# Strassen's seven products summed in three PSUM banks, with ScalarE copies in place of VectorE additions

## The chip, the core and the metric

The kernel runs on one core of a Trainium2 chip. The metric is the device time of one execution in microseconds (us). Engines are named as the profile names them: PE is TensorE (matmul), PEld its weight load, DVE VectorE, ACT ScalarE, POOL GpSimd, SP SyncE (which only issues DMAs here).

## What is computed

A transformer block in float32: T = 2048 tokens, width D = 1024, D_FF = 2816. The first two thirds (input projection, attention, pooling mixer, output projection) are not touched. The change lies in the gated MLP at the end, on the normalised tokens h:

```
u = h @ w_up                                   # (2048, 1024) @ (1024, 5632)
u = up[:-2]*conv_w[0] + up[1:-1]*conv_w[1] + up[2:]*conv_w[2] + conv_b   # along the tokens
gate, val = u[..., :D_FF], u[..., D_FF:]
return (silu(gate) * val) @ w_down             # (2048, 2816) @ (2816, 1024)
```

## The kernel before

Each float32 operand of a matmul is split into a high and a low part, and a product is the sum of three matmuls: high x high, high x low, low x high. The splits are a cast on ScalarE (`wh_*`, `gh`, `wdh`) and a subtraction on GpSimd or VectorE (`wl_*`, `gl`, `wdl`).

**Parts and units.** The MLP works through the tokens in three parts (`PARTS`): 640, 768 and 640 tokens. For each part it goes through 22 units j; a unit computes 128 columns of the gate half and 128 of the value half of `u`, as a 2x2 block product: two halves of the contraction, the gate and the value block of w_up on the stationary side, two halves of the tokens (N = 322, 386, 322 columns) on the moving side. Winograd's form of Strassen's product needs seven products, named 1 to 7, of 12 matmuls each (four blocks k of 128 rows by three splits; L1156), on sums of blocks: s1 to s4 of the weights, t1 to t4 of the tokens.

**The seven products before.** Each has a bank of its own out of five `pp` banks in turn, in the order 1, 6, 2, 7, 5, 4, 3. ScalarE copies product 1 to `p1s` (L1163). VectorE adds the rest: w1 = 6 + p1s (L1165), c11 = 2 + p1s (L1167), w7 = 7 + w1 (L1169), c22 = 5 + w7 (L1171), w1 = 5 + w1 (L1172), c21 = w7 - 4 (L1174), c12 = 3 + w1 (L1176). c11 and c12 are the two token halves of the gate block `ug`, c21 and c22 those of the value block `uv`.

**What runs beside a unit.** The loop in which a unit's matmuls are written steps other generators, so that their instructions stand between: `gen_w` prepares the weights of the next unit (casts on ScalarE L1033, sums and subtractions on GpSimd L1035 to L1055; seven buffers for the seven operands); `gen_gate` does the convolution and gate of the unit before (ScalarE L1199, VectorE L1202 and L1205 for each half, silu L1208, the product of the halves on VectorE L1212, its split `gh` on ScalarE L1219 and `gl` on VectorE L1221); `gen_down` multiplies the gate of unit j-2 with w_down, five or six token tiles by two column halves, each a group of three matmuls into one of three `py` banks (L1233), emptied by a VectorE addition to `y` (L1238; the first group of a part by a copy on ScalarE, L1236). Only in part 1, VectorE also multiplies w_down by the gate vector (`wds`, L56) and splits it (L1123, with ScalarE L1122). In units 2 to 6 of part 1 one VectorE addition of 128x1024 brings in the residual (L1312); in parts 2 and 3 halves of it (L1257). The first unit of parts 2 and 3 (`kmajor`) runs its seven products side by side over k; the second unit has no down-projection between its products, which begins with the third.

Each engine carries out its instructions in the order in which they were put on it; a scheduler sets that order by the program's dependences, so that an edit in `gen_up` also moves what stands beside it. A bank or buffer is written again when its last reader is done.

Of the kernel before, what the change touches and what calls it, by code (L numbers as in the profile page):

```python
# [14 lines left out]
ALU = mybir.AluOpType  # L15
# [32 lines left out]
class InOrder:  # L48
    """An engine whose instructions stay in the order in which they are written."""
# [15 lines left out]
def hybrid_block(ctx: ExitStack, tc: tile.TileContext, x, c, w_ada, b_ada, norm1_g, w_in,  # L65
# [58 lines left out]
    # =============== mixer input projection ===============  # L124
    with tc.tile_pool(name="p1", bufs=1) as p1, \
            tc.tile_pool(name="ps1", bufs=1, space=PSUM) as ps1:
        # columns of w_in: q, k, v first (their space is free first), then u
# [173 lines left out]
        # scale and shift of the first norm; the first tokens' norm beside them  # L301
# [18 lines left out]
        # weights, split, in the order of use  # L320
# [19 lines left out]
        # 1/count at the clipped edges  # L340
# [108 lines left out]
        def gen_tr(tok, qhl, khl):  # L449
            """q as (hi, lo), k as (hi, hi) and (lo, one), transposed"""  # L450
# [25 lines left out]
        def windows(b, us, res):  # L476
            """column i is token t0 - 8 + i, at column 8 + i of u; the last block has 8 more"""
# [74 lines left out]
        def gen_early_max():  # L552
            """the row maxima of the first unit over the keys of the blocks that are done"""
# [75 lines left out]
    # =============== attention and output projection ===============  # L629
    ctx3 = ctx.enter_context(ExitStack())  # L630
    with tc.tile_pool(name="po", bufs=1, side="right", reuse_waits="tile") as po, \
# [8 lines left out]
        # per key tile: [v_lo 0 | v_hi 0 | ones | v_hi 1 | v_lo 1]  # L640
# [185 lines left out]
        def gen_out(c_, half, wait=0):  # L826
            """x1 = x + pool half, then x1 += attention half."""
# [17 lines left out]
        def gen_ln2(t, x1, junk, hts, bank, stat, wait):  # L845
            """normalised x1, transposed"""
# [31 lines left out]
        # the last chunk's output projection: the pool half first, in banks that the attention leaves  # L878
# [67 lines left out]
        # =============== gated conv MLP: Winograd's form of Strassen's product ===============  # L946
# [12 lines left out]
        def gen_ops(p, res):  # L959
            """the moving operands of part p, split"""  # L960
# [10 lines left out]
            for k in range(4):  # L971
# [35 lines left out]
                G.tensor_tensor(out=t2, in0=t2, in1=b21, op=ALU.subtract)  # L1007
# [7 lines left out]
        def gen_w(p, j, res):  # L1015
            """the stationary operands of one pair of column tiles, split, in the order of use"""
# [22 lines left out]
            yield  # L1039
            s1, s2 = raw2(f"s1_{p}_{j}"), raw2(f"s2_{p}_{j}")  # L1040
# [3 lines left out]
            yield  # L1044
            split("a12", a12)
# [54 lines left out]
    with tc.tile_pool(name="p3", bufs=1, reuse_waits="tile") as p3, \  # L1100
# [5 lines left out]
        def gen_wd(p, j, n, tag=""):  # L1106
            """w_down times the gate, split: worked out with the first part, kept in DRAM for the others"""
# [18 lines left out]
            else:  # L1126
# [7 lines left out]
        PROD = (("1", "a11", "b11"), ("6", "s2", "t2"), ("2", "a12", "b21"), ("7", "s3", "t3"),  # L1134
                ("5", "s1", "t1"), ("4", "a22", "t4"), ("3", "s4", "b22"))

        def gen_up(p, j, kmajor, res):
            o0, no, N = PARTS[p]
# [5 lines left out]
            w1 = p3.tile([P, 386], F32, tag="w1", name=f"w1{p}_{j}", bufs=1)[:, 0:N]  # L1144
            w7 = p3.tile([P, 386], F32, tag="w7", name=f"w7{p}_{j}", bufs=1)[:, 0:N]
            res.append((p, j, ug, uv))

            def bank(i):
                py = kmajor and i < 2
                return ps3_.tile([P, 512], F32, tag="py" if py else "pp", name=f"pp{PROD[i][0]}{p}_{j}",  # L1150
                                bufs=3 if py else 5)[:, 0:N]

            def prod(ps, i, k):
                (ah, al), (bh, bl) = w[PROD[i][1]], o[PROD[i][2]]
                for m, (l_, r_) in enumerate(((ah, bh), (ah, bl), (al, bh))):
                    mm = PE.matmul(ps, l_[:, k], r_[:, k, 0:N], start=k == 0 and m == 0, stop=k == 3 and m == 2)  # L1156
                    if kmajor:
                        tc.keep_in_program_order(mm)
                    yield

            def add(i, ps):
                if i == 0:
                    S.copy(out=p1s, in_=ps)  # L1163
# [14 lines left out]
            if kmajor:  # L1178
# [4 lines left out]
                for i in range(7):  # L1183
                    add(i, banks[i])
# [226 lines left out]
```

## Time and profile before

| | |
|---|---|
| median of 3 runs | 2740.19 us (2736.31 to 2745.56) |
| span of the profiled execution | 2741.8 us |
| TensorE busy | 2594.1 us (95%) |
| VectorE busy | 2370.5 us (86%) |
| ScalarE busy | 1475.5 us (54%) |
| GpSimd busy | 1767.0 us (64%) |
| MLP, part 1 from its first unit | from 1283 us |
| 12 steady units of part 1 | 1478.41 to 1731.10 us |
| 17 steady units of part 2 | 1842.02 to 2235.18 us |
| 17 steady units of part 3 | 2378.57 to 2706.33 us |

No separate device time of the profiled execution is recorded; its span stands for it. A start is in us from the beginning of the span. Instructions of one engine overlap at their ends, so the distance from one start to the next can be shorter than an instruction.

### The profile page before, as it was taken

How to read it: one execution, taken by the hardware profiler on the slowest of the kernel's cores; microseconds unless marked ns; L12 is line 12 of the kernel's file. 1: busy time of each engine (PE TensorE's matmuls, PEld its weight loads, DVE VectorE, ACT ScalarE, POOL GpSimd, SP SyncE). 2: the span in 40 equal slices, each digit the busy share in tenths (PEclk: the TensorE clock that was granted, in tenths of full speed). 3: DMA queues.
4: the chain of work that ended last, by engine and by line, in shares of the span. 5: the costliest groups of instructions: out<-in, count | busy, mean ns of one | idle time of the engine just before them, and what ended most of it. 6: DMA issues, size and time to landing. Idle time of an engine off the chain costs nothing.

```text
span 2741.8 us, 39488 instructions
## 1 busy us (share of the span) xinstructions
PE 2594.1 (95%) x13439; PEld 2242.1 (82%) x13439; DVE 2370.5 (86%) x3526; ACT 1475.5 (54%) x2656; POOL 1767.0 (64%) x1397
## 2 busy tenths in 40 slices
PE   5899989999999999999899999899999998999999
PEld 5788867777776767767888888789999997999998
DVE  7778688989999998887999999978888888898886
ACT  5566457777778777775533443543333334533342
POOL 1222146556657666565888888697777776988883
PEclk9899989999999999999999999999999999999999
DMA  9685374331221222225444444443333224433332
GB/s 291 232 258 179 99 239 149 106 95 60 64 80 55 71 72 76 80 64 179 151 130 133 128 130 123 145 132 105 100 104 100 93 87 132 147 123 120 106 110 93
DMA packets 318164, 338.65 MB, mean 124 GB/s; under 512 B 24655, under 2 KB 226329, under 8 KB 317961
## 3 DMA queue, kind: packets, MB, share of 16 engines
q1 hardware_dynamic: 316953, 332.31, 38.4%
q0 software_dynamic: 1008, 3.81, 0.5%
q8 instruction: 106, 1.74, 0.3%
q14 instruction: 97, 0.79, 0.1%
HBM read 249.42 MB, written 86.63 MB: 123 GB/s over the span
## 4 chain that ended last, share of the span: by engine, by line
PE 36%; DVE 13%; issue 3%; ACT 1%; POOL 1%; POOLq 0%; DVEq 0%; ACTq 0%
PE pp L1156 23%; PE py L1233 13%; DVE y L1238 3%; DVE ac L1202 2%; DVE ac L1205 2%; DVE b L993 1%; DVE t L993 1%; ACT ac L1199 1%; PE pl L1354 1%; DVE wds L56 0%; DVE wdl L1123 0%; DVE ac L1212 0%; DVE ug L1176 0%; DVE uv L1171 0%; DVE uv L1174 0%
## 5 line engine op out<-in xcount | busy, mean ns | idle before, releaser
L1035 POOL TENSOR_TENSOR wl_s<-s,wh_s 128x512 fp32r<-128x512 f32 x260 | 390.3, 1502 | 187.8 <-ACT wh_s L1033 186.6
L1238 DVE TENSOR_TENSOR y<-py,y 128x512 f32<-128x512 f32 x620 | 418.5, 682 | 95.5 <-PE py L1233 94.8
L741 POOL TENSOR_TENSOR acc<-acc,ph 128x512 f32<-128x512 f32 x352 | 463.4, 1316 | 41.0 <-ACT ph L735 15.7
L1156 PE MATMUL pp<-t,wh_s 128*128 128x322 f32 (+1 forms) x1584 | 390.2, 322 | 7.0 <-DVE x L1072 3.2
L737 DVE TENSOR_TENSOR pl<-S,ph 128x512 fp32r<-128x512 f32 x512 | 348.7, 684 | 38.5 <-ACT S L736 31.5
L735 ACT ACTIVATE ph<-S 128x512 fp32r<-128x512 f32 x512 | 307.3, 600 | 131.9 <-PE S L732 116.2
L694 DVE TENSOR_REDUCE mx<-pmx 128x1 f32<-128x512 f32 x500 | 338.1, 681 | 27.0 <-PE pmx L692 25.2
L1035 POOL TENSOR_TENSOR wl_a<-wr,wh_a 128x512 fp32r<-128x512 f32 x195 | 312.9, 1605 | 22.7 <-ACT wh_a L1033 22.6
L1233 PE MATMUL py<-wdh,gh 128*128 128x512 f32 x674 | 275.7, 409 | 47.1 <-DVE y L1238 40.6
L736 ACT ACTIVATE S<-S 128x512 f32<-128x512 f32 x512 | 306.4, 598 | 0.0
L1156 PEld LDWEIGHTS pp<-t,wh_s 128*128 128x128 f32 x1584 | 282.2, 190 | 27.8 <-DVE t L993 4.1
L1033 ACT CAST wh_s<-s 128x512 fp32r<-128x512 f32 x264 | 161.9, 617 | 226.8 <-PE pp L1156 197.0
L1156 PE MATMUL pp<-b,wh_a 128*128 128x322 f32 (+1 forms) x1056 | 267.9, 323 | 1.3 <-DVE b L993 0.8
L1233 PE MATMUL py<-wdh,gl 128*128 128x512 f32 x674 | 268.8, 399 | 0.0
L1233 PE MATMUL py<-wdl,gh 128*128 128x512 f32 x674 | 268.8, 399 | 0.0
L1156 PE MATMUL pp<-t,wl_s 128*128 128x322 f32 (+1 forms) x792 | 254.3, 321 | 0.0
L724 PE MATMUL B<-pl,vt 128*128 128x512 f32 x512 | 210.5, 411 | 6.2 <-DVE pl L737 6.0
L1033 ACT CAST wh_a<-wr 128x512 fp32r<-128x512 f32 x198 | 122.3, 618 | 165.6 <-PE pp L1156 158.4
L723 PE MATMUL A<-ph,vt 128*128 128x512 f32 x512 | 204.7, 408 | 5.2 <-ACT ph L735 5.2
L692 PE MATMUL pmx<-kA,qa 128*128 128x512 f32 x500 | 203.3, 408 | 3.9 <-DMA kA<-k_scr 3.0
L739 POOL TENSOR_TENSOR acc<-ph,ph 128x512 f32<-128x512 f32 x32 | 41.3, 1290 | 256.8 <-ACT ph L735 226.9
L732 PE MATMUL S<-qb,kB 65*128 65x512 f32 x512 | 202.8, 402 | 1.1 <-ACT qb L702 0.8
(273 smaller groups left out, 6784.4 us busy)
## 6 DMA issues: line engine op xcount, KB each, us to landing
wr<-in_w_up_dram SPq DMA_DIRECT2D x132, 512.0 KB
wdh<-wd_scr SPq DMA_DIRECT2D x88, 256.0 KB
wdl<-wd_scr SPq DMA_DIRECT2D x88, 256.0 KB
stage<-in_w_ada_dram SPq DMA_DIRECT2D x36, 512.0 KB
x_scr<-x SPq DMA_DIRECT2D x48, 256.0 KB
wds<-in_w_down_dram SPq DMA_DIRECT2D x44, 256.0 KB
wd_scr<-wdh SPq DMA_DIRECT2D x44, 256.0 KB
wd_scr<-wdl SPq DMA_DIRECT2D x44, 256.0 KB
```

The costliest lines, as they stand in the source:

```text
L694: V.tensor_reduce(out=mx[:, qt, j:j + 1], in_=ps, axis=AX.X, op=ALU.max)
L723: PE.matmul(A, vt[:, kt, 192 * a:192 * a + P], ph, start=kt == 0, stop=kt == NKT - 1)
L724: PE.matmul(B, vt[:, kt, 64 + 64 * a:192 + 64 * a], pl, start=kt == 0, stop=False)
L735: S.activation(out=ph, in_=s, func=AF.Exp, scale=0.125)
L736: S.activation(out=s, in_=s, func=AF.Exp, scale=0.125)
L737: V.tensor_tensor(out=pl, in0=s, in1=ph.bitcast(F32), op=ALU.subtract)
L741: G.tensor_tensor(out=acc, in0=acc, in1=ph.bitcast(F32), op=ALU.add)
L1033: S.copy(out=hf, in_=src)
L1035: eng.tensor_tensor(out=lf, in0=src, in1=hf.bitcast(F32), op=ALU.subtract)
L1156: mm = PE.matmul(ps, l_[:, k], r_[:, k, 0:N], start=k == 0 and m == 0, stop=k == 3 and m == 2)
L1233: PE.matmul(ps, l_[:, ts_], r_, start=i == 0, stop=i == 3 * len(js) - 1)
L1238: V.tensor_tensor(out=ys[t][:, ns], in0=ps, in1=ys[t][:, ns], op=ALU.add)
```

## The change

A unit uses three banks, X, Y and W, and lets TensorE do four of the sums by accumulating on what a bank already holds: X takes product 1, then 6, then 5, then 3; W takes 7, then 4; Y takes 2. The values are read out between: X after 1 is `p1s`; X after 6 is 1 + 6, copied to `u2s`; W after 7 is copied to `w7`; X after 5 is 1 + 6 + 5, to which VectorE adds w7 for c22; W after 4 is added to u2s for c21; X after 3 is c12, copied straight to `ug`. The operand t4 changes its sign, so that product 4 is added. The order of products becomes 1, 2, 6, 7, 5, 4, 3, and `gen_w` prepares a12 ahead of s2. Units with `kmajor` keep seven banks and the old sums.

```
# gen_ops
-                G.tensor_tensor(out=t2, in0=t2, in1=b21, op=ALU.subtract)
+                G.tensor_tensor(out=t2, in0=b21, in1=t2, op=ALU.subtract)
# gen_w
+            split("a12", a12)
+            yield
             s1, s2 = raw2(f"s1_{p}_{j}"), raw2(f"s2_{p}_{j}")
             E.tensor_tensor(out=s1, in0=a21, in1=a22, op=ALU.add)
             E.tensor_tensor(out=s2, in0=s1, in1=a11, op=ALU.subtract)
             split("s2", s2)
-            yield
-            split("a12", a12)
             yield
# gen_up
+            def prod(ps, nm, k, first=True):
+                (ah, al), (bh, bl) = w[PROD[nm][0]], o[PROD[nm][1]]
                 for m, (l_, r_) in enumerate(((ah, bh), (ah, bl), (al, bh))):
+                    mm = PE.matmul(ps, l_[:, k], r_[:, k, 0:N], start=first and k == 0 and m == 0,
+                                   stop=k == 3 and m == 2, skip_group_check=not first)
...
-            else:
-                for i in range(7):
-                    ps = bank(i)
-                    for k in range(4):
-                        yield from prod(ps, i, k)
-                    add(i, ps)
+            X, Y, W = bank("x"), bank("y"), bank("w")
+
+            def run(ps, nm, first):
+                for k in range(4):
+                    yield from prod(ps, nm, k, first)
+
+            yield from run(X, "1", True)
+            S.copy(out=p1s, in_=X)
+            yield from run(Y, "2", True)
+            add(c11, Y, p1s)
+            yield from run(X, "6", False)
+            S.copy(out=u2s, in_=X)
+            yield from run(W, "7", True)
+            S.copy(out=w7, in_=W)
+            yield from run(X, "5", False)
+            add(c22, X, w7)
+            yield from run(W, "4", False)
+            add(c21, W, u2s)
+            yield from run(X, "3", False)
+            S.copy(out=c12, in_=X)
```

How this moves instructions is seen on two engines. First ScalarE in a steady unit of part 1 (j = 4), from the copy of product 1 to the last weight cast; in a name the number behind the tile's name is the part, then the unit. Before:

```order
L1163 COPY p1s0_4_14927<-pp10_4_14930 128x322
L1208 ACTIVATE ac00_3_14939<-ac00_3_14939 128x640
L1033 CAST wh_s20_5_14993<-s2_0_5_14990 128x512
L1122 CAST wdh0_3_0_15013<-wds0_3_0_14921 128x512
L1219 CAST gh0_3_15072<-ac00_3_14939 128x640
L1033 CAST wh_a120_5_15021<-wr0_5_0_14934 128x512
L1122 CAST wdh0_3_1_15085<-wds0_3_1_14923 128x512
L1033 CAST wh_s30_5_15055<-s3_0_5_15053 128x512
```

And with the change (the line numbers are those of the changed kernel: L1187, L1191 and L1193 are the three copies, L1217 silu, L1228 the gate's high part `gh`):

```order
L1187 COPY p1s0_4_14907<-ppx0_4_14910 128x322
L1217 ACTIVATE ac00_3_14921<-ac00_3_14921 128x640
L1033 CAST wh_a120_5_14969<-wr0_5_0_14916 128x512
L1122 CAST wdh0_3_0_14989<-wds0_3_0_14901 128x512
L1228 CAST gh0_3_15050<-ac00_3_14921 128x640
L1033 CAST wh_s20_5_15001<-s2_0_5_14998 128x512
L1191 COPY u2s0_4_14908<-ppx0_4_14910 128x322
L1122 CAST wdh0_3_1_15063<-wds0_3_1_14903 128x512
L1033 CAST wh_s30_5_15034<-s3_0_5_15032 128x512
L1193 COPY w70_4_14909<-ppw0_4_14912 128x322
```

The cast of a12 now stands ahead of `gh` and that of s2 behind it; behind that comes the copy of X to `u2s`, and two casts later that of W to `w7`.

Second, VectorE in the same unit, from the sum with product 7 to that with product 4. Before (L1312 is the residual, L1238 a sum of the down-projection):

```order
L1169 TENSOR_TENSOR w70_4_14929<-pp70_4_15032,w10_4_14928 128x322
L1238 TENSOR_TENSOR y0_1_14465<-py0_2_1_1_15065,y0_1_14465 128x512
L1238 TENSOR_TENSOR y0_2_14466<-py0_2_2_1_15092,y0_2_14466 128x512
L1171 TENSOR_TENSOR uv0_4_14926<-pp50_4_15061,w70_4_14929 128x322
L1172 TENSOR_TENSOR w10_4_14928<-pp50_4_15061,w10_4_14928 128x322
L1312 TENSOR_TENSOR y0_2_14466<-y0_2_14466,xr0_4_15037 128x1024
L1238 TENSOR_TENSOR y0_3_14467<-py0_2_3_1_15109,y0_3_14467 128x512
L1174 TENSOR_TENSOR uv0_4_14926<-w70_4_14929,pp40_4_15101 128x322
```

And the same stretch with the change (L1164 is the addition of `gen_up`, L1247 a sum of the down-projection, L1321 the residual):

```order
L1247 TENSOR_TENSOR y0_1_14455<-py0_2_1_1_15043,y0_1_14455 128x512
L1247 TENSOR_TENSOR y0_2_14456<-py0_2_2_1_15070,y0_2_14456 128x512
L1164 TENSOR_TENSOR uv0_4_14906<-ppx0_4_14910,w70_4_14909 128x322
L1321 TENSOR_TENSOR y0_2_14456<-y0_2_14456,xr0_4_15016 128x1024
L1247 TENSOR_TENSOR y0_3_14457<-py0_2_3_1_15085,y0_3_14457 128x512
L1164 TENSOR_TENSOR uv0_4_14906<-ppw0_4_14912,u2s0_4_14908 128x322
```

The sums w7 and w1 are gone; c22 is added from bank X, with the residual behind it, and c21 from bank W.

## Rows read from the trace of the kernel before

**Rows 1.** The head of the page: span, then busy time, share, instructions

```profile
span 2741.8 us, 39488 instructions
...
PE 2594.1 (95%) x13439; PEld 2242.1 (82%) x13439; DVE 2370.5 (86%) x3526; ACT 1475.5 (54%) x2656; POOL 1767.0 (64%) x1397
```

**Rows 2.** Stage windows: us, busy of PE, PEld, DVE, ACT, POOL, PEclk

```profile
1347.08:1478.41 131.33, 118.40 (x674) 106.94 (x675) 129.34 (x166) 51.32 (x86) 112.65 (x68) 1.00 0.45 139
1478.41:1731.10 252.69, 238.92 (x1373) 217.30 (x1373) 247.98 (x325) 102.53 (x170) 206.63 (x133) 1.00 0.41 125
...
2378.57:2706.33 327.76, 327.76 (x1934) 306.07 (x1934) 291.76 (x400) 131.35 (x205) 279.99 (x188) 1.00 0.35 110
```

**Rows 3.** TensorE's waits in part 1 (total, times, longest)

```profile
PE py L1233 <- DVE y L1238: 26.7, 36, 1.5
```

**Rows 4.** VectorE's waits in twelve steady units of part 1

```profile
DVE ac L1202 <- ACT ac L1199: 4.7, 12, 0.4
```

**Rows 5.** VectorE's groups in the same units: times, busy, mean ns

```profile
L1212 DVE TENSOR_TENSOR ac<-ac,ac 128x640 f32<-128x640 f32 x12 | 21.8, 1815 | 0.0
...
L1165 DVE TENSOR_TENSOR w<-pp,p1s 128x322 f32<-128x322 f32 x12 | 5.8, 482 | 0.0
```

**Rows 6.** VectorE's timeline, one unit of part 1: start, length, instruction

```profile
1600.12 0.48 DVE L1174 TENSOR_TENSOR uv<-w,pp 128x322 f32<-128x322 f32 x1
...
1603.24 1.51 DVE L1205 SCALAR_TENSOR_TENSOR ac<-uv,cols,ac 128x640 f32<-128x640 f32 x1
...
1606.51 1.77 DVE L56 TENSOR_TENSOR wds<-wds,gate 128x512 f32<-128x512 f32 x1
...
1608.81 0.87 DVE L1205 SCALAR_TENSOR_TENSOR ac<-ug,cols,ac 128x640 f32<-128x640 f32 x1
...
1610.20 0.68 DVE L56 TENSOR_TENSOR wds<-wds,gate 128x512 f32<-128x512 f32 x1
1610.80 0.48 DVE L1165 TENSOR_TENSOR w<-pp,p1s 128x322 f32<-128x322 f32 x1
1611.20 1.82 DVE L1212 TENSOR_TENSOR ac<-ac,ac 128x640 f32<-128x640 f32 x1
```

**Rows 7.** ScalarE's timeline in the same unit

```profile
1604.75 0.42 ACT L1163 COPY p1s<-pp 128x322 f32<-128x322 f32 x1
...
1613.05 0.73 ACT L1219 CAST gh<-ac 128x640 fp32r<-128x640 f32 x1 [1.52 <-DVE ac L1212]
1613.68 0.62 ACT L1033 CAST wh_a<-wr 128x512 fp32r<-128x512 f32 x1
```

**Rows 8.** TensorE's timeline: first matmuls of products, one down

```profile
1802.77 0.52 PE L1156 MATMUL pp<-t,wh_s 128*128 128x386 f32 x2
...
1823.22 0.80 PE L1233 MATMUL py<-wdh,gh 128*128 128x512 f32 x1 [2.90 <-ACT y L1236]
...
2330.93 0.45 PE L1156 MATMUL pp<-t,wh_s 128*128 128x322 f32 x2
...
2580.11 0.46 PE L1156 MATMUL pp<-t,wh_s 128*128 128x322 f32 x2
...
2585.71 0.47 PE L1156 MATMUL pp<-b,wh_s 128*128 128x322 f32 x2
```

**Rows 9.** VectorE's timeline, a unit of part 3: c21

```profile
2585.91 0.49 DVE L1174 TENSOR_TENSOR uv<-w,pp 128x322 f32<-128x322 f32 x1
```

**Rows 10.** GpSimd: one group in part 1's steady units, then a timeline row

```profile
L1035 POOL TENSOR_TENSOR wl_s<-s,wh_s 128x512 fp32r<-128x512 f32 x48 | 74.6, 1553 | 39.7 <-ACT wh_s L1033 39.7
...
1611.04 1.30 POOL L1035 TENSOR_TENSOR wl_s<-s,wh_s 128x512 fp32r<-128x512 f32 x1 [3.31 <-ACT wh_s L1033]
```

**Rows 11.** ScalarE's timeline: gh in units of parts 2 and 3

```profile
1807.69 0.84 ACT L1219 CAST gh<-ac 128x768 fp32r<-128x768 f32 x1 [0.62 <-DVE ac L1212]
...
2330.85 0.73 ACT L1219 CAST gh<-ac 128x640 fp32r<-128x640 f32 x1
...
2576.60 0.73 ACT L1219 CAST gh<-ac 128x640 fp32r<-128x640 f32 x1 [1.11 <-DVE ac L1212]
```

More of the change, by code (lines that the diff above doesn't have):

```diff
@@ L1133, in hybrid_block @@
         G1, O0, O1, O2 = 2, 0, 1, 3
-        PROD = (("1", "a11", "b11"), ("6", "s2", "t2"), ("2", "a12", "b21"), ("7", "s3", "t3"),
-                ("5", "s1", "t1"), ("4", "a22", "t4"), ("3", "s4", "b22"))
+        PROD = {"1": ("a11", "b11"), "6": ("s2", "t2"), "2": ("a12", "b21"), "7": ("s3", "t3"),
+                "5": ("s1", "t1"), "4": ("a22", "t4"), "3": ("s4", "b22")}
         def gen_up(p, j, kmajor, res):
@@ L1143, in gen_up, with bank @@
             p1s = p3.tile([P, 386], F32, tag="p1s", name=f"p1s{p}_{j}", bufs=1)[:, 0:N]
-            w1 = p3.tile([P, 386], F32, tag="w1", name=f"w1{p}_{j}", bufs=1)[:, 0:N]
+            u2s = p3.tile([P, 386], F32, tag="w1", name=f"u2s{p}_{j}", bufs=1)[:, 0:N]
             w7 = p3.tile([P, 386], F32, tag="w7", name=f"w7{p}_{j}", bufs=1)[:, 0:N]
             res.append((p, j, ug, uv))
[L1148 to L1154, printed above, removed]
+            c11, c12, c21, c22 = ug[:, 0:N], ug[:, N:2 * N], uv[:, 0:N], uv[:, N:2 * N]
+            def bank(nm, tag="pp"):
+                return ps3_.tile([P, 512], F32, tag=tag, name=f"pp{nm}{p}_{j}",
+                                 bufs=3 if tag == "py" else 5)[:, 0:N]
+            def prod(ps, nm, k, first=True):
+                (ah, al), (bh, bl) = w[PROD[nm][0]], o[PROD[nm][1]]
                 for m, (l_, r_) in enumerate(((ah, bh), (ah, bl), (al, bh))):
-                    mm = PE.matmul(ps, l_[:, k], r_[:, k, 0:N], start=k == 0 and m == 0, stop=k == 3 and m == 2)
+                    mm = PE.matmul(ps, l_[:, k], r_[:, k, 0:N], start=first and k == 0 and m == 0,
+                                   stop=k == 3 and m == 2, skip_group_check=not first)
                     if kmajor:
@@ L1159, in prod, with add @@
                     yield
[L1161 to L1176 removed]
+            def add(out, ps, b):
+                V.tensor_tensor(out=out, in0=ps, in1=b, op=ALU.add)
@@ L1178, in gen_up @@
             if kmajor:
-                banks = [bank(i) for i in range(7)]
+                banks = {nm: bank(nm, "py" if i < 2 else "pp") for i, nm in enumerate("1627543")}
                 for k in range(4):
-                    for i in range(7):
-                        yield from prod(banks[i], i, k)
-                for i in range(7):
-                    add(i, banks[i])
-            else:
-                for i in range(7):
-                    ps = bank(i)
-                    for k in range(4):
-                        yield from prod(ps, i, k)
-                    add(i, ps)
+                    for nm, ps in banks.items():
+                        yield from prod(ps, nm, k)
@@ new lines, in gen_up @@
+                S.copy(out=p1s, in_=banks["1"])
+                add(u2s, banks["6"], p1s)
+                add(c11, banks["2"], p1s)
+                add(w7, banks["7"], u2s)
+                add(c22, banks["5"], w7)
+                add(u2s, banks["5"], u2s)
+                add(c21, banks["4"], w7)
+                add(c12, banks["3"], u2s)
+                return
+            X, Y, W = bank("x"), bank("y"), bank("w")
+            def run(ps, nm, first):
+                for k in range(4):
+                    yield from prod(ps, nm, k, first)
```

12 lines of the change are left out of this document (removed).

## The prediction

> **What bounds the kernel now.** The page's head first [rows 1]: TensorE is busy for 95% of the span, VectorE for 86%. That is an average over stages, so next come the stage windows [rows 2]. In the steady stretch of part 3 TensorE is busy without a gap (327.76 of 327.76 us) and VectorE is not (291.76); part 2, with its wider products, is of the same kind. Nothing that only unloads VectorE can gain there. Seventeen units of part 3 take 327.76 us, 19.28 each, and this is the matmul time of a unit of 322 columns. Part 1 has the same matmuls and is another case. Its twelve steady units take 252.69 us, 21.06 each, with VectorE busy for 247.98 of them and TensorE for 238.92. Its six units ahead of these take 131.33, 21.89 each, with VectorE busy for 129.34. The waits agree: in part 1 TensorE stands 26.7 us in 36 waits, all for the y additions that empty the py banks [rows 3], and VectorE idles 4.7 us in twelve units, all for ScalarE [rows 4]. So VectorE sets the pace of 18 units, TensorE that of the rest, and the change can earn only in part 1: 12 x (21.06 - 19.28) + 6 x (21.89 - 19.28) = 37 us at the very most.
>
> **What it takes from VectorE.** Four additions a unit leave it (L1165, L1169, L1172, L1176), busy for 0.48 us each by L1165's mean [rows 5], but overlapped with the next: from the start of L1165 to that of L1212 it is 1611.20 - 1610.80 = 0.40 [rows 6]. All four have the same 322 columns, so 1.6 us together. VectorE's own sum falls to 21.06 - 1.6 = 19.46 us, still a hair above TensorE's 19.28.
>
> **What it gives ScalarE.** Three copies more a unit, at the 0.42 us of the p1s copy [rows 7]: 1.3 us on an engine that is busy 102.53 us in twelve units (8.5 of 21 us each) [rows 2]. The load is nothing. TensorE's own instructions are the same in number and length.
>
> **What it adds: four waits on TensorE.** Each bank is written again one product after it was read. X+=6 waits for the p1s copy, W+=4 for the w7 copy, X+=3 for the VectorE addition c22, and in each case the reader has a product's time, with the downs between, to be done. The one that matters is X+=5, behind u2s, because of what stands ahead of u2s on ScalarE: gh and wh_s2 (the ScalarE order above). gh waits for the product of the two gate halves on VectorE (L1212 before), which ends the convolution of the unit before, which begins with that unit's c21. So a ring closes: c21, convolution, gh, u2s, products 5 and 4, c21 again. I work out its length in part 1. From the start of c21 (1600.12) to gh (1613.05) it is 12.93 us [rows 6, 7]; the c12 addition that VectorE has in between (0.40) goes, so 12.53. gh to the next start is 0.63, the cast behind it 0.62, the copy 0.42 [rows 7]: 1.67, in whose full lengths the signals are contained. From the start of product 5 to that of product 3 TensorE needs 2585.71 - 2580.11 = 5.60 us where it does not wait [rows 8], and c21 starts 0.20 us after that [rows 9]. Sum: 12.53 + 1.67 + 5.60 + 0.20 = 20.0 us. This is above 19.46, so the ring and not VectorE's sum sets the new pace. It contains two-input VectorE work that stretches when GpSimd works beside it: L1212 takes 1815 ns on average in part 1, while L1205, as large, takes 0.87 us at 1608.81, where GpSimd is idle: its instruction at 1611.04 starts after 3.31 us of waiting [rows 5, 6, 10]. I add 0.3 us for such shifts: **20.3 us**. The bounds of the unit are 19.46 (no ring) and 21.8 (rival D).
>
> The gain of part 1: 12 x (21.06 - 20.3) = 9.1 us. The six units ahead carry the addition of the residual too, between c22 and c21, inside the ring's TensorE leg; by 0.3 us more than the plain ones, 20.6: 6 x (21.89 - 20.6) = 7.7. Together 16.8 us.
>
> **The same wait in parts 2 and 3.** In a steady unit of part 3 gh starts at 2576.60 and product 5 at 2580.11 [rows 8, 11]: u2s would be done 1.7 us after gh, 1.8 us early; here a second cast of 0.62 us comes ahead of it, so 1.2. No wait. In part 2, with 386 columns in place of 322, product 5 comes later still. The second unit of each part is different: it has no down-projection between its products, so product 5 comes early, while gh hangs on a first unit whose sums all come late. In part 2 product 5 starts at 1802.77 and gh at 1807.69 [rows 8, 11]; u2s would end at 1809.4, and TensorE stand 6.6 us. Much is given back, since today it stands 2.90 us a little later for the first y copies [rows 8], and catches up against work that is there anyway: I take 2 us (bounds 0 and 6.6). In part 3 it is 2330.93 against 2330.85 + 1.7 [rows 8, 11]: 1.6 us. The start of part 1 gets 0.5, and the three ends of parts, whose gate chain loses the 0.40 us of c12 each, give 1.2 back. Net cost: 2 + 1.6 + 0.5 - 1.2 = 2.9 us.
>
> **Sum.** The profiled execution's span is 2741.8 us [rows 1], 1.6 above the median of the three runs, 2740.19. 2741.8 - 16.8 + 2.9 = 2727.9 on the profile's basis; less part of the 1.6 that the profile lies high, **2727 us**.
>
> **The Trainium skill against the trace.** What the trace shows: the 1.82 us of L1212 begin 0.16 us into a GpSimd subtraction of 1.30 us [rows 6, 10], whose mean in twelve units is 1.55 us [rows 10]; VectorE and GpSimd together are busy for 247.98 + 206.63 us in 252.69 [rows 2], far more than the stretch: the two do run at once, slowed, and not only by turns. The Trainium skill's page "SBUF — State Buffer" (section "Who interferes with whom") states that a VectorE instruction with two SBUF inputs and a GpSimd instruction that reads SBUF hold a shared port by turns, and that the loser blocks for the whole instruction. By that rule time that VectorE gets free goes to waiting for GpSimd, and part 1 hardly shortens; the trace agrees in that L1205 is short where GpSimd is idle, and not in the full exclusion. It makes rival C.
>
> **The rivals.**
> B, the ring does not bind: u2s comes in time, since the shorter unit leaves the convolution less to share with GpSimd. For it: half a us of the ring is all that decides. Units take 19.46, and 20.29 with a residual: 18 x 1.6 = 28.8 saved, 2.9 lost, about 2715 us.
> C, nothing comes of it: the additions that leave read one of their inputs from PSUM, keep their 0.48 us on average [rows 5] and are not the work that stretches; all of that is left. GpSimd's 17.2 us a unit is then packed against less VectorE time, and a unit stays at 20.9 to 21. By the formula below that gains 4 to 6 us, against a cost of 2.9: 2738 us.
> D, the other side: the ring is longer than I have it. Its convolution contains an L1205 of 0.87 us and a wds of 0.68 that were short since GpSimd idled there; their fellows beside GpSimd take 1.51 and 1.77 [rows 6]. If GpSimd, whose work for the next unit now comes in another order (a12 ahead of gh on ScalarE, s2 behind it), fills that hole and idles elsewhere, the two stretch by 0.64 and 1.09 us, and the ring is 21.8 us. With 0.3 more for the six units ahead, as above, part 1 gains 12 x (21.06 - T) + 6 x (21.59 - T) at a unit of T; from T = 21.1 on that no longer pays the 2.9 us, and the change costs time. At 21.8 it loses 10.1, with the 2.9 13 us: 2754; at 21.5, 7.6: 2748. I put D at 2750.
>
> **How the numbers follow.** Chances: forecast (2722 to 2734) 0.45, B 0.20, C 0.19, D 0.16. What a measurement of this kernel can tell from no change is about 0.3%, 8.2 us: faster is below 2732, slower above 2748. Of the forecast 0.4 of 0.45 is faster, and with B's 0.2, less a little for its tail, 0.57; slower is D, less its lower end, and the tail of C where the second unit of part 2 pays its full wait, 0.14; the rest 0.29. The range for 8 in 10 goes from a little under B, 2712, to where C ends and D begins, 2745.
>
> **What would show it.** In the trace of the changed kernel: TensorE waits in part 1 put down to ScalarE's u2s (or to the pp bank behind it), about 0.9 us a unit, with the y waits of [rows 3] mostly gone; VectorE idle, about 0.8 us a unit; units of about 20.3 us, and unchanged 19.3 us in part 3; one wait of several us in the second unit of part 2. If units of part 1 are at 19.5, B is right; if VectorE is as busy as before with longer convolution instructions, C; if the u2s waits are over 1.5 us a unit, D. The forecast is wrong altogether if the banks' other three waits show up in every unit of parts 2 and 3, which have no room for any.

## The result, and the profile after

The changed kernel takes 2761.93 us (median of 4 runs, 2761.34 to 2775.07), the kernel before 2739.31 beside it: a ratio of 1.0089, 95% interval 1.0064 to 1.0113. It is slower by 23 us, where 2727 was forecast.

The head of the changed kernel's page, as in [rows 1] (the span, then busy time, share and instructions):

```profile
span 2759.4 us, 39247 instructions
...
PE 2593.6 (94%) x13439; PEld 2246.9 (81%) x13439; DVE 2310.2 (84%) x3270; ACT 1548.8 (56%) x2848; POOL 1749.2 (63%) x1397
```

VectorE lost 256 instructions and 60 us of busy time, and the span grew by 17.6 us. The changed kernel's first unit began 4.5 us earlier than before's, which the edit does not touch, so from there on it lost 22.1. The copy of product 1 to p1s comes once a unit, so its starts can serve as marks. Between marks at units where they stand alike in both programs, part 1 loses 6.1 us, and the two changes from part to part lose 7.3 and 7.1:

```
                                               before    changed
first copy to unit 9 of part 1                 193.29     196.17   +2.9
nine steady units of part 1                    189.50     192.71   +3.2
unit 18 of part 1 to unit 4 of part 2          196.92     204.25   +7.3
sixteen steady units of part 2                 370.35     370.98   +0.6
unit 20 of part 2 to unit 5 of part 3          162.65     169.77   +7.1
sixteen units of part 3                        308.50     309.47   +1.0
```

Stage windows of the changed kernel (columns as in [rows 2]): nine steady units of part 1, and the second unit of part 3:

```profile
1476.79:1669.50 192.71, 177.03 (x1028) 162.99 (x1027) 187.91 (x208) 87.79 (x155) 153.18 (x100) 1.00 0.40 123
2339.49:2354.73 15.24, 14.77 (x78) 14.54 (x79) 9.16 (x9) 8.50 (x17) 12.80 (x10) 0.79 0.34 115
```

A steady unit is 192.71 / 9 = 21.41 us, against 21.06 before. VectorE is recorded as busy for 187.91 of the 192.71 us, with 1.6 us of additions less in each unit. TensorE's waits from the MLP's first unit to the end (answer to [rows 3], which covers part 1):

```profile
PE ppx L1157 <- ACT u2s L1191: 44.5, 24, 6.2
PE py L1242 <- DVE y L1247: 10.8, 13, 2.2
PE ppx L1157 <- ACT p1s L1187: 8.7, 3, 5.2
```

The y waits of part 1 are gone, and 53 us of waits for the copies u2s and p1s have come, the u2s waits of the nine steady units being 15.7 of them. Three of them on TensorE's timeline: one of a steady unit of part 1, and those of the second units of parts 2 and 3:

```profile
1615.41 0.57 PE L1157 MATMUL ppx<-t,wh_s 128*128 128x322 f32 x2 [1.73 <-ACT u2s L1191]
...
1814.65 1.01 PE L1157 MATMUL ppx<-t,wh_s 128*128 128x386 f32 x2 [6.23 <-ACT u2s L1191]
...
2339.96 0.91 PE L1157 MATMUL ppx<-t,wh_s 128*128 128x322 f32 x2 [5.24 <-ACT p1s L1187]
```

And what ScalarE did in the first and the last of these places (answer to [rows 7]):

```profile
1610.46 0.74 ACT L1217 ACTIVATE ac<-ac 128x640 f32<-128x640 f32 x1 [4.77 <-DVE ac L1214]
1611.10 0.60 ACT L1033 CAST wh_a<-wr 128x512 fp32r<-128x512 f32 x1
...
1613.79 0.73 ACT L1228 CAST gh<-ac 128x640 fp32r<-128x640 f32 x1 [1.51 <-DVE ac L1221]
1614.42 0.61 ACT L1033 CAST wh_s<-s 128x512 fp32r<-128x512 f32 x1
1614.94 0.42 ACT L1191 COPY u2s<-ppx 128x322 f32<-128x322 f32 x1
...
2338.34 0.74 ACT L1217 ACTIVATE ac<-ac 128x640 f32<-128x640 f32 x1 [7.28 <-DVE ac L1214]
2338.98 0.60 ACT L1033 CAST wh_a<-wr 128x512 fp32r<-128x512 f32 x1
2339.49 0.42 ACT L1187 COPY p1s<-ppx 128x322 f32<-128x322 f32 x1
```

In part 1 u2s (1614.94) stands behind gh and wh_s2, as the prediction said. In part 3 p1s (2339.49) stands behind silu, which waits 7.28 us for the convolution; the prediction saw this only for u2s.

Next, VectorE's and GpSimd's timelines in the same unit of part 1, as [rows 6, 10]:

```profile
1607.28 1.31 DVE L1211 SCALAR_TENSOR_TENSOR ac<-ug,cols,ac 128x640 f32<-128x640 f32 x1
...
1609.11 1.31 DVE L1214 SCALAR_TENSOR_TENSOR ac<-ug,cols,ac 128x640 f32<-128x640 f32 x1
...
1611.55 0.48 DVE L1164 TENSOR_TENSOR ug<-ppy,p1s 128x322 f32<-128x322 f32 x1
1611.95 1.80 DVE L1221 TENSOR_TENSOR ac<-ac,ac 128x640 f32<-128x640 f32 x1
```

```profile
1607.87 1.88 POOL L1035 TENSOR_TENSOR wl_a<-wr,wh_a 128x512 fp32r<-128x512 f32 x1
1611.78 1.29 POOL L1035 TENSOR_TENSOR wl_a<-wr,wh_a 128x512 fp32r<-128x512 f32 x1 [2.04 <-ACT wh_a L1033]
1615.11 1.30 POOL L1035 TENSOR_TENSOR wl_s<-s,wh_s 128x512 fp32r<-128x512 f32 x1 [2.04 <-ACT wh_s L1033]
```

Read the two together. GpSimd's operation of 1611.78 ends at 1613.07. VectorE's product of the halves (L1221) starts at 1611.95 and ends at 1613.75: 0.68 us after that. It was on the engine for 1.80 us, and as a run below shows it needs 0.81 alone. The same at 1609.11: GpSimd ends at 1607.87 + 1.88 = 1609.75, VectorE at 1610.42, 0.67 later. And the other way round: GpSimd's operation of 1607.87 starts while VectorE's L1211 runs, which ends at 1608.59; it takes 1.88 us where the next takes 1.29, and ends 1.16 after L1211. Whoever comes second waits, and the wait is recorded as busy.

All of the nine units' trace is like this. 72 VectorE instructions with both operands in SBUF start while a GpSimd operation runs, with 0.62 to 1.24 us of it left, and end 0.68 us (54 of 128x640: 0.677 to 0.685) or 0.55 us (18 of 128x512: 0.546 to 0.552) after it, however much was left. The 18 others start while GpSimd stands and take 0.67 to 0.68 us. 54 GpSimd operations start while such an instruction runs and end 1.15 to 1.17 us after it; the 45 others take 1.29 to 1.30. So the two take turns, and in what follows a turn is such an instruction of either engine.

GpSimd itself stands twice a unit, for casts that ScalarE has behind silu and behind gh (waits of the nine units):

```profile
POOL wl_a L1035 <- ACT wh_a L1033: 18.4, 9, 2.0
POOL wl_s L1035 <- ACT wh_s L1033: 18.3, 9, 2.0
```

And VectorE's groups, first in the twelve steady units of before (more of the view of [rows 5]), then in these nine:

```profile
L1123 DVE TENSOR_TENSOR wdl<-wds,wdh 128x512 fp32r<-128x512 f32 x24 | 23.4, 976 | 0.0
...
L1205 DVE SCALAR_TENSOR_TENSOR ac<-uv,cols,ac 128x640 f32<-128x640 f32 x12 | 18.1, 1510 | 0.0
...
L1221 DVE TENSOR_TENSOR gl<-ac,gh 128x640 fp32r<-128x640 f32 x12 | 15.8, 1313 | 0.0
L1205 DVE SCALAR_TENSOR_TENSOR ac<-ug,cols,ac 128x640 f32<-128x640 f32 x12 | 10.4, 870 | 0.0
```

```profile
L1123 DVE TENSOR_TENSOR wdl<-wds,wdh 128x512 fp32r<-128x512 f32 x18 | 22.1, 1228 | 0.0
L1221 DVE TENSOR_TENSOR ac<-ac,ac 128x640 f32<-128x640 f32 x9 | 16.3, 1808 | 0.0
L1214 DVE SCALAR_TENSOR_TENSOR ac<-uv,cols,ac 128x640 f32<-128x640 f32 x9 | 16.2, 1805 | 0.3
L1230 DVE TENSOR_TENSOR gl<-ac,gh 128x640 fp32r<-128x640 f32 x9 | 14.5, 1608 | 0.0
...
L1214 DVE SCALAR_TENSOR_TENSOR ac<-ug,cols,ac 128x640 f32<-128x640 f32 x9 | 11.8, 1312 | 0.0
```

The second step of the convolution is L1205 before and L1214 now: 1510 and 1805 ns for the value half, 870 and 1312 for the gate half. The product of the halves (L1212 before, L1221 now) keeps its 1.81 us; wdl and gl are longer as well.

### The profile page after: what moved, and what is told of

Same layout as the page of the kernel before. It is cut to its first block, busy times and chain, and to the rows that moved or that the text cites. A ratio compares the mean times of both kernels' runs of the same rounds, so it can differ in the third digit from the quotient of the medians.

```text
span 2759.4 us, 39247 instructions
## 1 busy us (share of the span) xinstructions
PE 2593.6 (94%) x13439; PEld 2246.9 (81%) x13439; DVE 2310.2 (84%) x3270; ACT 1548.8 (56%) x2848; POOL 1749.2 (63%) x1397
## 4 chain that ended last, share of the span: by engine, by line
PE 37%; DVE 13%; issue 2%; ACT 2%; POOL 1%; DMA 1%; SPq 0%; ACTq 0%; POOLq 0%; DVEq 0%
PE ppx L1157 13%; PE py L1242 13%; PE ppw L1157 7%; PE ppy L1157 3%; DVE ac L1214 3%; DVE ac L1211 2%; DVE y L1247 2%; DVE wds L56 2%; DVE ac L1221 1%; DVE b L993 1%; DVE t L993 1%; PE pl L1363 1%; ACT wh_s L1033 0%; ACT hb L977 0%; POOL wl_s L1035 0%
## 5 line engine op out<-in xcount | busy, mean ns | idle before, releaser
L1247 DVE TENSOR_TENSOR y<-py,y 128x512 f32<-128x512 f32 x620 | 415.5, 683 | 152.2 <-PE py L1242 149.5
L735 ACT ACTIVATE ph<-S 128x512 fp32r<-128x512 f32 x512 | 307.0, 600 | 129.5 <-PE S L732 117.6
L1157 PE MATMUL ppx<-t,wh_s 128*128 128x322 f32 (+1 forms) x1024 | 258.5, 332 | 53.2 <-ACT u2s L1191 44.5
L1242 PE MATMUL py<-wdh,gh 128*128 128x512 f32 x674 | 269.7, 400 | 13.4 <-DVE y L1247 10.8
L1157 PEld LDWEIGHTS ppx<-t,wh_s 128*128 128x128 f32 x1024 | 185.5, 195 | 71.1 <-ACT u2s L1191 50.9
L731 PE MATMUL S<-qa,kA 128*128 128x512 f32 x512 | 202.2, 398 | 0.0
L1217 ACT ACTIVATE ac<-ac 128x640 f32<-128x640 f32 (+1 forms) x66 | 51.2, 776 | 208.7 <-DVE ac L1214 208.7
```

Source lines behind the costliest of these rows:

```text
L735: S.activation(out=ph, in_=s, func=AF.Exp, scale=0.125)
L1157: mm = PE.matmul(ps, l_[:, k], r_[:, k, 0:N], start=first and k == 0 and m == 0, stop=k == 3 and m == 2, skip_group_check=not first)
L1242: PE.matmul(ps, l_[:, ts_], r_, start=i == 0, stop=i == 3 * len(js) - 1)
L1247: V.tensor_tensor(out=ys[t][:, ns], in0=ps, in1=ys[t][:, ns], op=ALU.add)
```

## The experiments

All are timed beside the kernel before. "Unit" is a steady unit of part 1, from nine of them. e1, e3 and e11 leave out a part of the computation, as their texts say; the others compute all of it. The edits are shown shortened.

```
                              median    ratio, 95% interval       unit
the change                    2761.93   1.0089  1.0064-1.0113    21.41
e1  banks of their own        2746.82   1.0012  1.0000-1.0025    21.41
e2  gh behind u2s, w7         2731.42   0.9964  0.9951-0.9977    20.34
e3  no GpSimd low parts       2685.13   0.9795  0.9775-0.9814    19.39
e4  the order alone           2753.68   1.0045  1.0030-1.0060    21.43
e5  before, casts first       2731.66   0.9961  0.9946-0.9976    20.89
e6  e2, silu behind a12       2732.09   0.9965  0.9951-0.9979    20.21
e7  one GpSimd sum more       2753.81   1.0047  1.0031-1.0063    21.55
e8  e6, two lows on VectorE   2740.50   0.9997  0.9982-1.0011    20.56
e9  before, two on VectorE    2742.40   1.0014  1.0004-1.0024    21.30
e10 change, two on VectorE    2753.76   1.0055  1.0039-1.0072    21.20
e11 e4 without wdl            2708.98   0.9890  0.9874-0.9907    19.63
e12 e2, old second units      2728.03   0.9959  0.9945-0.9973    20.34
e13 e2, a12 and s2 on VectorE 2741.95   1.0008  0.9997-1.0019    20.96
```

**e1, banks of their own.** The theory under test first was the prediction's own ring.

```
...
+            X = bank("6")
             yield from run(X, "6", False)      # run() now starts each sum anew
             S.copy(out=u2s, in_=X)
...                                             # a bank for each of the seven
```

> The readers of the change (four ScalarE copies, three VectorE additions, same order on ScalarE), but each of the seven products in a bank of its own, so that no product waits for the reader of the one before it; the sums that TensorE makes by accumulating are left out. Theory R (the ring: TensorE waits for copies that stand behind gh and silu on ScalarE): the 44.5 us of u2s waits and 8.7 of p1s waits are gone, a steady unit of part 1 falls from 21.40 to 19.5 to 20.5 us, the second unit of part 3 from 15.9 to about 10 us, and the total is 2712 to 2728. Theory G (VectorE's remaining work stretches beside GpSimd and fills what is freed): units of part 1 stay at 20.8 to 21.1, only the starts of parts are repaired, total 2735 to 2742.

Its nine steady units (window; then two groups of VectorE; then TensorE's waits):

```profile
1497.17:1689.86 192.69, 179.60 (x1028) 163.01 (x1027) 189.26 (x208) 86.86 (x155) 153.14 (x100) 1.00 0.40 123
```

```profile
L1219 DVE SCALAR_TENSOR_TENSOR ac<-uv,cols,ac 128x640 f32<-128x640 f32 x9 | 16.3, 1806 | 0.3
...
L1235 DVE TENSOR_TENSOR gl<-ac,gh 128x640 fp32r<-128x640 f32 x9 | 14.5, 1615 | 0.0
```

```profile
PE py L1247 <- DVE y L1252: 13.1, 18, 1.0
```

No wait for a copy is left in these units, and they are as long as in the change, 21.41 us. The y waits are back in their place. So theory R fell for the steady units: TensorE does wait there for the ring that the prediction built, 1.73 us a unit, but these waits only take the place of the y waits (13.1 us in nine units, 1.5 each). Theory G had units of 20.8 to 21.1 us and a total of 2735 to 2742, so it fell short too. What the waits cost lies elsewhere. From the first mark to the last the change takes 17.9 us more than e1: 4.6 up to unit 9 of part 1, 4.8 from part 1 to part 2, 8.1 from part 2 to part 3, and 0.4 in the rest.

**e4, the order alone.**

```
-        PROD = (("1", "a11", "b11"), ("6", "s2", "t2"), ("2", "a12", "b21"), ...
+        PROD = (("1", "a11", "b11"), ("2", "a12", "b21"), ("6", "s2", "t2"), ...
 # and in gen_w split("a12", a12) ahead of s1, s2, split("s2", s2), as in the change
```

> The kernel before with nothing but the order of the change: products 1, 2, 6, 7, 5, 4, 3 and a12 prepared ahead of s2; seven banks, seven VectorE additions, one copy. Both theories: no change, 2735 to 2743, units of part 1 at 21.0 to 21.1. If the new order of GpSimd's work is what stretches VectorE's, units of part 1 are at 21.3 or more and the total is 2744 to 2750.

Its steady units (window; three groups of VectorE; GpSimd's waits):

```profile
1497.87:1690.73 192.86, 180.25 (x1028) 162.87 (x1027) 189.33 (x245) 76.96 (x127) 153.31 (x100) 1.00 0.40 123
```

```profile
L1123 DVE TENSOR_TENSOR wdl<-wds,wdh 128x512 fp32r<-128x512 f32 x18 | 15.8, 878 | 0.0
L1205 DVE SCALAR_TENSOR_TENSOR ac<-uv,cols,ac 128x640 f32<-128x640 f32 x10 | 15.1, 1511 | 0.0
...
L1221 DVE TENSOR_TENSOR gl<-ac,gh 128x640 fp32r<-128x640 f32 x9 | 11.8, 1310 | 0.0
```

```profile
POOL wl_a L1035 <- ACT wh_a L1033: 18.4, 9, 2.0
POOL wl_s L1035 <- ACT wh_s L1033: 18.4, 9, 2.0
```

The order alone costs 12 us, for which the prediction counted nothing. In before GpSimd stood 3.31 us behind silu [rows 10] and 0.22 for wh_a12; now it stands 2.04 behind silu and 2.04 behind gh. And e4 against e1 is the cleanest pair of all: the same order, a bank for each product in both, the same two GpSimd waits of 2.04 us, seven additions on VectorE and one ScalarE copy here, three additions and four copies there. 21.43 and 21.41 us. **Four additions less, 1.6 us, shorten a unit by 0.02.** Where they went stands in the groups: gl is 1310 ns in e4 and 1615 in e1, the second step of the value half 1511 and 1806. The 90 VectorE instructions with both operands in SBUF that start in the nine units add up to 116.3 us in e4 and to 129.5 in e1: 1.5 us a unit more, for the same work.

**e3, GpSimd's low parts left out.**

```
-                eng.tensor_tensor(out=lf, in0=src, in1=hf.bitcast(F32), op=ALU.subtract)
+                if E is V:                       # the first unit of all
+                    V.tensor_tensor(out=lf, in0=src, in1=hf.bitcast(F32), op=ALU.subtract)
+                else:
+                    l_ = h_
```

> The changed kernel without GpSimd's subtractions of the weights' low parts (seven of its eleven operations a unit; the high part is multiplied in their place). Theory R with GpSimd's stretch in the ring: the way from c21 to gh falls from 13.68 us to 9 to 11, the ring is shorter than TensorE's 19.4 us, steady units of part 1 are at 19.4 with no u2s wait. If the ring's length has nothing to do with GpSimd, the way stays at 13 to 13.7 us and the unit at 21.4. The start of part 3 keeps its p1s wait if that hangs on the convolution's place alone.

```profile
1492.61:1667.09 174.48, 174.48 (x1027) 162.69 (x1026) 150.26 (x208) 87.82 (x154) 48.21 (x36) 1.00 0.44 136
```

```profile
L1218 DVE SCALAR_TENSOR_TENSOR ac<-uv,cols,ac 128x640 f32<-128x640 f32 x9 | 8.0, 885 | 0.3
...
L1225 DVE TENSOR_TENSOR ac<-ac,ac 128x640 f32<-128x640 f32 x9 | 7.3, 808 | 0.0
```

TensorE is busy throughout, 19.39 us a unit, and the same two instructions of VectorE that took 1805 and 1808 ns in the change take 885 and 808. They need no more than that; half of their time was waiting for GpSimd. The way from c21 to gh is 10.40 us in one of these units (1584.59 to 1594.99) against 13.68 in the change, within what the text expected.

**e2, gh behind the copies.** Two edges of order on ScalarE, the whole computation:

```
+                    behind(S.activation(out=t_, in_=t_, func=AF.Silu), p1s copy)
+            behind(S.copy(out=gh, in_=ag), u2s copy, w7 copy)
```

> The changed kernel, complete, with two edges of order on ScalarE: silu behind the p1s copy, and gh behind the u2s and w7 copies of the unit that runs beside it. Theory R: the same as with banks of their own, within 4 us, since X+=5 and X+=6 find their copies done; u2s waits under 5 us in all; total 2712 to 2728. Theory G: units of part 1 at 20.8 to 21.1, total 2735 to 2745. If gh, now later, makes VectorE stand at gl, VectorE shows an idle time for gh that it has not in the changed kernel.

```profile
1490.31:1673.40 183.09, 179.47 (x1028) 162.96 (x1027) 178.21 (x208) 87.73 (x154) 161.88 (x100) 1.00 0.40 130
```

```profile
POOL wl_a L1035 <- ACT wh_a L1033: 18.4, 9, 2.0
```

Between the two theories: 20.34 us and 30 us less than the change. With gh out of its way the cast of s2 is early, GpSimd's second wait is gone, and with it 1.07 us of the unit. The u2s waits are gone as well, but e1 showed that a unit is no shorter without them.

**e5, e6, e7, or whether GpSimd alone sets the pace (theory P).** In e5 the kernel before gets the order "silu behind the cast of s2, gh behind that of a12"; in e6 e2 gets silu behind the cast of a12 and gh behind that of s2 as well; in both the gate's steps are written eight matmuls later. In e7, `s3` is computed twice in the kernel before:

```
 # e5                                            # e7
+ behind(silu, casts["s2"])                      + for _ in range(2):
+ behind(gh, casts["a12"])                           E.tensor_tensor(out=s3, in0=a11, in1=a21, ...)
- if n % 8 == 4:
+ if n % 8 == 4 and n >= 12:
      step(gate)
```

> The kernel before, complete (seven banks, seven VectorE additions), with an order on ScalarE alone: silu behind the cast of s2, gh behind the cast of a12, and the gate's steps written eight matmuls later. Theory P (in part 1 GpSimd sets the pace: its eleven operations, stretched where VectorE reads two operands from SBUF beside them, and the times it stands for casts that wait behind silu and gh): GpSimd's wait of 3.31 us a unit for wh_s2 falls under 0.5, a steady unit of part 1 from 21.06 to 19.5 to 20.4, total 2715 to 2730. Theory V (VectorE's own sum bounds the unit, as forecast): VectorE has as much to do as before, so the unit stays at 21.0 to 21.1 and the total at 2736 to 2745.

> The changed kernel, complete, with gh behind the copies u2s and w7 as in the run before it, and silu behind the cast of a12 as well. Theory P: GpSimd's last wait of 2.04 us a unit (for wh_a12 behind silu) goes, a steady unit of part 1 falls from 20.34 to TensorE's 19.4 to 19.8, total 2712 to 2722. Theory V: VectorE is busy for 97% of a unit of 20.34 us and keeps all its work, so nothing is gained, 2728 to 2735.

> The kernel before with one GpSimd operation more in each unit: the sum s3 is computed twice. Theory P: steady units of part 1 go from 21.06 by the length of one, 1.3 to 1.8 us, to 22.3 to 22.9, parts 2 and 3 are not touched in their steady units, total +25 to +33 us. Theory V: GpSimd is idle for 3.5 us a unit and takes the operation there, units of part 1 grow by under 0.5 us, total under +10 us.

e7 speaks against theory P. An operation more lengthened the unit by 0.5 us and not by 1.3 to 1.8; GpSimd took most of it out of its wait for wh_s2, 3.31 us before and 1.8 now (GpSimd's waits in e7's nine units; the total grew by 12.5 us, a little more than V's 10):

```profile
POOL wl_s L1035 <- ACT wh_s L1033: 14.5, 8, 2.0
```

e5 and e6 can't decide it, since the waits only moved: GpSimd stands 3.4 us a unit in e5 (1.8 for wh_a, 1.6 for wh_s) where it stood 3.5 before, and 1.9 in e6 where it stood 2.04 in e2. The units are 0.17 and 0.13 us shorter. Still, e5 is faster than before by 10 us in all, with all seven additions on VectorE.

**e8, e9, e10, or whether the sum of both engines' turns is a floor (theory X).** Low parts of s3 and s1 on VectorE in part 1, on top of e6, of before and of the change:

```
-        VS = ((), (), ())
+        VS = (("s3", "s1"), (), ())
```

> The run before it (the changed kernel with silu and gh behind the copies and casts), and in part 1 the low parts of s3 and s1 are subtracted by VectorE and not by GpSimd. Theory X (VectorE's operations with two SBUF inputs and GpSimd's operations take turns, so a unit of part 1 is no shorter than the sum of both, about 20.2 to 20.8 us): two operations of 1.25 us on GpSimd become two of 0.60 on VectorE, the sum falls by 1.3, and the unit from 20.21 to 19.4 to 19.7, where TensorE ends it; total 2716 to 2726. Theory V (VectorE's own sum of recorded times bounds the unit): VectorE gets 1.2 us more, unit 21.2 to 21.5, total 2748 to 2756.

> The kernel before, and in part 1 the low parts of s3 and s1 on VectorE. VectorE then has 42 operations less than none to spare: it is recorded as busy for 98% and gets 1.2 us more a unit. Theory X: the sum of both engines' turns falls by 1.3 us, unit from 21.06 to 19.8 to 20.3, total 2718 to 2730. Theory V: unit 22.2 to 22.5, total 2760 to 2768.

> The changed kernel as it is, without any edge of order, and in part 1 the low parts of s3 and s1 on VectorE. Theory X: unit from 21.40 to 19.8 to 20.5; what the second units of parts 2 and 3 lose stays, total 2733 to 2745. Theory R (the ring through u2s as forecast, lengthened): the convolution stands beside less GpSimd work, too, but VectorE has 1.2 us more between c21 and gh, unit 21 or more, total 2755 to 2765.

(In e9's text, two operations a unit are meant.) e8 and e9 came out between the theories, at 20.56 and 21.30 us; e10's unit, 21.20, is within R's and out of X's, and its total of 2753.76 just under R's. VectorE took 1.2 us more work a unit, and the units grew by 0.35, grew by 0.24 and shrank by 0.21. So VectorE's time is not simply added, as V has it, but the unit does not follow the sum of the turns down either; in e8 GpSimd had new waits, 1.8 us a unit for VectorE to read s1 before the next is written, and as many in e10 (2.6 in e9).

**e11, turns taken away.** Against e4, which it is in all else:

```
-                V.tensor_tensor(out=l_, in0=src, in1=h_.bitcast(F32), op=ALU.subtract)
+                l_ = h_
```

> The kernel with the order alone (seven additions on VectorE, unit 21.43 us), without the two subtractions of w_down's low parts a unit in part 1 (the high part is multiplied in their place): 1.2 us of VectorE work with two SBUF inputs, where the four additions that leave in the change are 1.6 us of work with one input from PSUM. Theory Y (VectorE's operations with two SBUF inputs and GpSimd's take turns; what reads PSUM runs beside GpSimd and is eaten by the next turn): taking 1.2 us of turns away shortens the unit by 1.2 to 2 us, to 19.4 to 20.2, although 1.6 us of additions shortened it by 0.03. Theory P (GpSimd and its waits for ScalarE alone): VectorE's work is not in the sum but through GpSimd's stretch, 21.0 to 21.4.

```profile
1478.10:1654.77 176.67, 176.56 (x1028) 162.92 (x1027) 169.72 (x226) 79.46 (x128) 155.67 (x101) 1.00 0.42 135
```

19.63 us a unit: 1.80 less than e4 for 1.2 us of work, and TensorE is busy for 176.56 of 176.67, so that more could not have shown. Four additions with one operand in PSUM were worth 0.02 us, two subtractions with both in SBUF 1.80. That is theory Y's forecast, and theory P, which had 21.0 to 21.4, fell. By VectorE's recorded times alone e11 could be explained too (two subtractions of 878 ns in e4 make 1.76 us); but the four additions, 1.6 us by the same account, were worth nothing.

**e12 and e13, towards a better kernel.** e12 gives the second units of parts 2 and 3 the seven banks of before, e13 puts the low parts of a12 and s2 on VectorE, both on top of e2:

```
 # e12                                           # e13
+            if j == 1 and p > 0:                -        VS = ((), (), ())
+                ... seven banks, seven sums     +        VS = (("a12", "s2"), (), ())
```

> The changed kernel with gh behind u2s and w7 and silu behind p1s, and in the second units of parts 2 and 3, which have no down-projection between their products, the seven banks and seven sums of before. If what is left of the waits there (u2s, 4.8 us in part 2) still costs time, the total falls by 3 to 5 us under that of the edges alone, to 2726 to 2729; if it is given back before the third unit is over, it is the same, 2730 to 2733.

> The changed kernel with the same two edges, and in part 1 the low parts of a12 and s2 (the two for which GpSimd waits) on VectorE. Theory Y: two turns of 1.25 us become two of 0.60, and GpSimd no longer waits for casts behind silu; unit from 20.34 to 19.4 to 19.9, total 2717 to 2725. Where the turns are not what holds a unit at 20.3 us but VectorE's own recorded time, it grows to 21.3 or more, total 2745 or more. In between (20.3 to 20.8) VectorE waits for casts or TensorE for c22, and the waits show it.

e12 takes 2728.03 us, the lowest median of the complete kernels, though its interval and those of e2, e5 and e6 overlap. By the marks it gains on e2 where it was meant to: 3.5 us from part 1 to part 2, 0.2 from part 2 to part 3. e13 did not do what it was meant to: 20.96 us a unit. GpSimd waits 6.2 us a unit until VectorE has read s2, whose buffer it needs for s4:

```profile
POOL s L1055 <- DVE wl_s L1035: 55.4, 9, 6.2
```

**What the turns add up to.** One more number can be added up from the traces: for how much of a steady unit at least one of the two engines had a turn on record, its waiting for the other included. "None" is the rest of the unit.

```
                     unit    a turn    none
before              21.06     19.77    1.29
the change          21.41     19.89    1.52
e1                  21.41     19.88    1.53
e4                  21.43     19.90    1.52
e2                  20.34     19.58    0.76
e6                  20.21     19.69    0.53
e8                  20.56     18.85    1.71
e9                  21.30     19.08    2.22
e10                 21.20     19.05    2.15
e11                 19.63     18.65    0.98
```

The turns alone come to more than TensorE's 19.39 us in the first six. The change left their sum nearly as it was (e1 and e4 agree to 0.02 us in both columns), and the new order made the pauses between them longer; e2 and e6 make the pauses shorter. In e8 to e10 the sum fell as theory X had it, and the pauses took it up.

## Why the prediction was wrong

**The step that failed: "VectorE's own sum falls to 21.06 - 1.6 = 19.46 us".** It took recorded busy time for work. In part 1 VectorE is the engine with hardly a gap, that much was right, but at least a fifth of its time it stands in front of GpSimd: in e3, without GpSimd's low parts, it is recorded as busy for 150.26 us in nine units and in the change, for the same work, for 187.91, 4.2 us a unit more. An addition from PSUM runs while GpSimd finishes its operation; if it goes, the next VectorE instruction with two SBUF operands comes to the same GpSimd operation earlier and stands longer. e1 against e4 measured the term: 0.02 us a unit, not 1.6. e11 shows what counts: 1.80 us for two instructions that take a turn, and then TensorE has no gap left.

**Rival C had the right mechanism for the steady units** (not the size: it had 20.9 to 21 us, and the order's share was missing), and it was held at 0.19 by a wrong reading: "247.98 + 206.63 us in 252.69", "far more than the stretch", so that the two "do run at once, slowed". Both numbers contain the waits of each for the other, and VectorE's additions from PSUM do run beside GpSimd, so they can add up to more than the stretch without two turns at once. [rows 6, 10] already showed it: L1212 at 1611.20 ends at 1613.02, 0.68 us behind GpSimd's end at 1611.04 + 1.30 = 1612.34. The Trainium skill's page "SBUF — State Buffer" (section "Who interferes with whom") has this as an exclusive lock for VectorE instructions with two SBUF inputs against GpSimd ones that read SBUF. The traces agree, in the full exclusion too: of the change's 128x640 instructions that met a GpSimd operation, all 54 ended 0.68 us after it, and an instruction of 1808 ns takes 808 once GpSimd's low parts are gone.

**The ring through u2s** was there (1.73 us a unit instead of 0.9), longer than computed mostly from c21 to gh, 13.68 us (c21 started at 1600.11, gh at 1613.79) against 12.53. The reason is of rival D's kind: three steps of the convolution meet more of GpSimd's work and are 0.20 (value half, first step), 0.30 (value half, second) and 0.44 us (gate half, second) longer on average; the wds that D counted as well kept its 0.68. From gh to product 5 it was 1.62 against 1.67 us, from there to the next c21 6.10 against 5.80. But it bound nothing that was not bound already: own banks have the same unit. So D's sign, u2s waits over 1.5 us a unit, came up, and D's total of 2754 is the nearest of the rivals', but that is luck: without these waits the unit is as long.

**The new order, counted at nothing,** costs 12 us in e4, about half of the loss. It stood in the list of ScalarE's instructions: a12 behind silu, s2 behind gh. What was not asked is who waits for these casts. It is GpSimd, which stands 4.1 us a unit for them where it stood 3.5, and the pauses in which neither engine has a turn grow by 0.23 us. That this is how the order costs 0.37 us a unit is read from the traces; no run parts the order of the products from that of the weights.

**The starts of parts** were put at 2.9 us net; against e1 the change loses 4.6 us at the start of part 1, which had 0.5 in the sum, and 12.9 at the two others. The wait of 6.23 us in part 2 was forecast at 6.6, but less was given back than the prediction took: from unit 1 to unit 4 of part 2 the change takes 70.4 us, e1 66.8, so 3.6 are left where 2 were forecast. In part 3 the p1s wait of 5.24 us was missed altogether: the prediction dismissed the other three waits with "the reader has a product's time", true in a steady unit, not where silu waits for a late first unit. Behind it TensorE was granted 0.79 of its clock over 15.24 us, a mean of its two levels; e1 was granted all of it over the same unit, which took 12.76 us.

**A slip that changes nothing above.** 19.28 us as TensorE's time for a unit is a mean with a shorter last stretch of 18.29 us in it; e3 shows 19.39.

**What was right:** parts 2 and 3 keep their steady units within 0.06 us, and the other waits don't appear in them.

**What stays open.** e2 and e6 stop at 20.2 to 20.3 us a unit, 0.9 above TensorE's time. Their turns fill 19.6 to 19.7 of it, so the turns alone keep them above 19.39; that fewer turns would bring them there is not shown, since e8 and e13, meant for it, made waits of their own.

## What to carry to other kernels

Before an engine's busy time is taken as the thing to shorten, compare the length of its instructions where another engine idles with that where it works; what differs is waiting, and relieving the engine will only lengthen it. Take away the work that collides, not the work that runs beside it; moving it to the other engine is not the same, as it can bring waits of its own. When an edit reorders one engine's queue, ask for each moved instruction who waits for it, on every engine, and do so at the first units of a loop as well as in the steady ones.

## What the runs showed of the hardware

VectorE instructions with two SBUF operands and GpSimd's took strict turns: in the nine units of the change 54 VectorE instructions of 128x640 ended 0.677 to 0.685 us after the GpSimd operation that they met, whether 0.62 or 1.14 us of it was left, and the profile counts the turn that is waited for as busy on the waiting engine. An addition of 128x322 with one operand in PSUM took 0.48 to 0.49 us on average in every one of these kernels. After TensorE had stood for 5.24 us its first pair of matmuls of 322 columns took 0.91 us, against 0.57 behind a wait of 1.73 and 0.45 without one; after 6.23 us the first pair of 386 columns took 1.01, against 0.52 without a wait [rows 8]. The granted clock of the stretch behind the wait of 5.24 us was 0.79: part of it at 1.2 GHz, the rest at 2.4.
